# A gated three-branch decoder layer on one core: the RWKV state chain in whole-array matmuls, another order of the projection jobs, shorter roots, copies on ScalarE

## The chip, the cores and the metric

The kernel runs on one core of a Trainium2 chip. The metric is the device time of one execution in microseconds (us), as the median of several runs. Five engines work beside each other: TensorE (PE, matmuls and transposes), VectorE (DVE), ScalarE (ACT), GpSimd (POOL) and SyncE (SP), which issues most DMA transfers. Each engine works its instructions off in the order in which they stand in its program, and waits on semaphores for the others' results.

## What is computed

One layer over x of shape (1, 256, 2048), float32, between two RMS norms:

```python
h = rms_norm(x, norm_w)
proj = h @ w_in                       # 2048 -> 16592 columns
g_qkv, g_z, g_b, g_a, r_feat, r_z, s_u, s_z, gate_logits = split(proj)
o_a = gdn_branch(...)     # gated delta rule, 8 heads of 128, conv of 4 taps on q, k, v, chunks of 64
o_b = rwkv7_branch(...)   # RWKV-7 time mixing, 16 heads of 64, token shift on r, k, v
o_c = s5_branch(...)      # diagonal state space model, 64 groups of 16
merged = sum_b sigmoid(gate_logits_b + gate_b) * (o_b @ w_branch_b)
x = x + merged @ w_out
return rms_norm(x, final_norm_w)
```

The RWKV recurrence is S_t = S_{t-1} (diag(w_t) - kk_t^T (a_t kk_t)) + v_t^T k_t, y_t = S_t r_t, with a state of 64 x 64 a head. Almost all arithmetic is in the three projections (w_in, w_branch, w_out); the branches are many small steps.

## The kernel before, in words

**Projections.** A weight block is loaded by a DMA into a tile raw (128 x 1024 floats). ACT rounds it to a shorter format (whi, line 260), DVE takes the rest (wlo = raw - whi, line 261). Each projection product is three matmuls: whi by the upper part of the activations, whi by the lower, wlo by the upper. They are the tiles mm in the profile, 128 x 256 each, some 8,000 of them, and they are the filling between all other work of PE. A unit is one raw tile (24 matmuls), and a job is the two units of one block of 128 output columns (one unit where the activations have 1024 rows). When a job's last matmul is done, its callback takes the result out of PSUM: got_conv (a causal convolution of 4 taps, one ACT operation and three DVE passes of 255, 254 and 253 columns, tiles gc), got_shift (the token shift of r, k, v), got_z, got_gate and so on.

**Branches as lanes.** The small steps of the branches are Python generators in lanes ("g" for a head of the delta rule, "r" for a pair of RWKV heads, "i" for the inversion that both share, "t", "g2", "r2"). After every second k block of a job, pump() lets each lane whose count is due take one step; the number that a step yields is how many pumps it waits for the next. All of PE's matmuls are kept in the written order (class InOrder). The instructions of the other engines are put in order by a scheduler, and so a change of one edit moves instructions at many places.

**Rounds.** For each of 8 rounds r, front() brings the jobs q, k, v of head r, its gate z, then r, k, v of RWKV pair r and its gate z. After the job gz a new delta-rule head begins (ag), after rz a new RWKV pair (ar). NG = 9 gate jobs follow the rounds (front_gates), then the jobs of the third branch's input (front_su). Then the pool of the first two branches is closed and the third branch begins: its parameters come by DMA (s5raw, s5ldt) into memory that was the first branches', DVE copies s5ldt (line 1289), and PE transposes them (s5t).

**The RWKV state chain.** One pair of heads lies on 128 partitions, head 0 on rows 0 to 63, head 1 on rows 64 to 127. For each of four chunks c of 64 steps it does: rc (KR by the state, from the second chunk; its sum on DVE is rpn, line 998), rd (rpn by Mr), whose result goes into UV (one half by ACT, one by DVE, line 1005), and re (BKt by UV, up to the third), from which DVE makes the next state MS (rMS, lines 1016 and 1018). Each of rc, rd and re is two matmuls of 64 rows and 64 columns of the array, one for each head, on two quadrants of it. ra, a part of the pair's preparation, and ryo, its output, are matmuls of one head each as well.

**Roots.** rsqrt (line 118) starts from an estimate out of the float's bits, in two operations, and improves it in two rounds of three or four; it is called for the norm of x at the start (2 columns), the norms in the branches and the last norm (1 column).

**Head.** x is loaded in four pieces (xs), its squares are summed on ACT and DVE, the root is taken, the diagonal matrices are made from it (sc, line 228), and PE multiplies x by them (xtp, a transpose and a scaling in one), which gives the activations hT.

Of the kernel before, what the change touches and what calls it, by code (L numbers as in the profile page):

```python
# [18 lines left out]
P = 128  # L19
# [17 lines left out]
def tile_trunk(  # L37
# [80 lines left out]
    def rsqrt(o, v, n, parts=P, pool=None):  # L118

        qi = small(n, parts, I32, pool, bufs=4)  # L120
        ve.tensor_scalar(out=qi, in0=v.bitcast(I32), scalar1=1, scalar2=None, op0=ALU.logical_shift_right)
# [4 lines left out]
        g = (9 / 64) ** 0.12  # L126
        for c in (g * g, 64 / 9 * g ** 10):
            if n <= 2:
                for e in range(n):
                    e = slice(e, e + 1)  # L130
                    ve.scalar_tensor_tensor(out=w[:, e], in0=o[:, e], scalar=o[:, e], in1=v[:, e], op0=ALU.mult,
                                            op1=ALU.mult)
            else:
                ve.tensor_tensor(out=w, in0=o, in1=o, op=ALU.mult)
                ve.tensor_tensor(out=w, in0=w, in1=v, op=ALU.mult)
            ve.scalar_tensor_tensor(out=t, in0=w, scalar=-10 / 3 * c, in1=w, op0=ALU.add, op1=ALU.mult)
            ve.scalar_tensor_tensor(out=o, in0=t, scalar=5 * c * c, in1=o, op0=ALU.add, op1=ALU.mult)
# [80 lines left out]
    squares(1, 0, 1024, 0, ve)  # L218
    squares(0, 1024, 2048, 1, se)
# [190 lines left out]
    hlw = cp.tile([P, 16], F32, name="hlw")  # L410

    def parameters():
# [7 lines left out]
        ve.tensor_scalar(out=oka, in0=pv("ka", 0, 8), scalar1=-1.0, scalar2=1.0, op0=ALU.mult, op1=ALU.add)  # L420
# [145 lines left out]
    def inverse(r, TMc):  # L566
# [12 lines left out]
        for e in range(2):  # L579
            ve.tensor_scalar(out=T16[:, :, 16 * e:16 * e + 16], in0=TMc, scalar1=rmask[:, e:e + 1], scalar2=None,  # L580
                             op0=ALU.mult)
# [65 lines left out]
        ve.tensor_copy(Y.rearrange("p u j -> p (u j)"), py[0:64, 0:P])  # L647
# [130 lines left out]
    def gdn_tail(h):  # L778
# [15 lines left out]
        ve.tensor_copy(ot[:, 0], po[:, 0:P])  # L794
# [74 lines left out]
    def rwkv_pair(i):  # L869
# [12 lines left out]
        ve.tensor_scalar(out=lw, in0=lw, scalar1=-RW_C, scalar2=-RW_C, op0=ALU.mult, op1=ALU.add)  # L882
        ve.tensor_scalar(out=av, in0=av, scalar1=0.5, scalar2=0.5, op0=ALU.mult, op1=ALU.add)
# [14 lines left out]
        ve.tensor_scalar(out=ns, in0=pr[0:2, 0:T], scalar1=EPS, scalar2=None, op0=ALU.add)  # L898
# [10 lines left out]
        ve.scalar_tensor_tensor(out=bt, in0=k, scalar=pv("kk", i), in1=av, op0=ALU.mult, op1=ALU.mult)  # L909
        for h, sl in ((0, 0), (1, 2)):  # L910
            hp = slice(64 * h, 64 * h + 64)
            ve.tensor_tensor(out=BK[hp, :, sl], in0=ch4(bt)[hp], in1=ch4(en)[hp], op=ALU.mult)
# [819 lines left out]
```

## Time and profile before

| | |
|---|---|
| time, median of 3 runs | 1202.21 us (1201.90 to 1202.29) |
| the profiled execution | 1201.51 us, of which the span from first to last instruction is 1199.8 us |
| PE busy | 1177.0 us (98%) |
| DVE, ACT, POOL busy | 955.3 (80%), 619.1 (52%), 52.4 us (4%) |
| mean granted TensorE clock | 0.998 |
| DMA | 203.98 MB, mean 170 GB/s |

The span has a head up to the first projection matmul at 17.46 us, a stretch in which PE streams, and a tail from its last matmul at 1191.0 us. The rounds lie between about 60 and 640 us, the third branch and the remaining projections behind them. PE is the busiest engine by far; a row "PE a <- DVE b" in the view of waits is time in which PE had nothing to do until DVE had made b. In the timeline the durations of PE's matmuls overlap, because a matmul is in the array while the next one starts; what one costs is read from start to start.

### The profile page before, as it was taken

Reading aid. Unit: us, or ns where it says so; the run is one execution under the profiler, and the core shown is the slowest. Engines: PE = TensorE matmul, PEld = TensorE weight load, DVE = VectorE, ACT = ScalarE, POOL = GpSimd, SP = SyncE. Lnnn points to the kernel's source line nnn. Section 1 sums busy time; section 2 is a strip of 40 time slices with the busy share of each in tenths; the row PEclk is TensorE's granted clock in tenths of the full one; section 3 lists DMA queues with packets and bytes.
Section 4 is the critical chain, followed back from the end, with each engine's and each line's share of the span. In section 5 each row is a group of like instructions: output and inputs, shape, how many; then the busy total and the mean of one; then the engine's idle time right before and its main releaser. Section 6 shows DMA issues by size and latency. Waiting matters only on the chain. (4 is left out here: it accounts for less than half of the span.)

```text
span 1199.8 us, 29344 instructions
## 1 busy us (share of the span) xinstructions
PE 1177.0 (98%) x11670; PEld 1124.6 (94%) x11670; DVE 955.3 (80%) x2527; ACT 619.1 (52%) x1188; POOL 52.4 (4%) x92
## 2 busy tenths in 40 slices
PE   5999999999999999999999999999999999999997
PEld 5999999999999999999999999999999999999887
DVE  6879888889898898977558978999998765555555
ACT  5455656565555656564544554544444554444443
POOL 1000000000000000000002011111100000000000
PEclk9999999999999999999999999999999999999999
DMA  6766555555555555555557776777767666667763
GB/s 189 194 176 180 152 136 146 139 157 133 152 149 137 150 137 150 133 146 144 147 159 203 192 193 179 186 185 191 187 175 192 176 182 187 180 190 240 238 197 116
DMA packets 384643, 203.98 MB, mean 170 GB/s; under 512 B 38825, under 2 KB 376186, under 8 KB 384122
## 3 DMA queue, kind: packets, MB, share of 16 engines
q1 hardware_dynamic: 382650, 199.61, 61.4%
q8 instruction: 92, 1.51, 0.5%
q0 software_dynamic: 1536, 1.58, 0.5%
q10 hardware_dynamic: 320, 0.93, 0.2%
q14 instruction: 45, 0.37, 0.1%
HBM read 195.88 MB, written 6.18 MB: 168 GB/s over the span
## 5 line engine op out<-in xcount | busy, mean ns | idle before, releaser
L62 PE MATMUL mm<-hT,whi 128*128 128x256 f32 (+1 forms) x4160 | 781.5, 288 | 0.5 <-ACT gate L1216 0.5
L62 PEld LDWEIGHTS mm<-hT,whi 128*128 128x128 f32 (+1 forms) x4160 | 644.4, 191 | 13.0 <-issue 1.2
L62 PE MATMUL mm<-hT,wlo 128*128 128x256 f32 (+1 forms) x2080 | 587.3, 282 | 0.4 <-DVE wlo L261 0.4
L260 ACT ACTIVATE whi<-raw 128x1024 fp32r<-128x1024 f32 (+1 forms) x346 | 364.7, 1055 | 361.7 <-PE mm L62 288.0
L261 DVE TENSOR_TENSOR wlo<-raw,whi 128x1024 fp32r<-128x1024 f32 (+1 forms) x346 | 421.6, 1219 | 150.1 <-ACT whi L260 148.3
L62 PEld LDWEIGHTS mm<-hT,wlo 128*128 128x128 f32 (+1 forms) x2080 | 396.4, 191 | 0.6 <-DVE wlo L261 0.6
L62 PE MATMUL mm<-oT,whi 128*128 128x256 f32 x768 | 140.4, 283 | 0.0
L62 PEld LDWEIGHTS mm<-oT,whi 128*128 128x128 f32 x768 | 118.9, 191 | 0.4 <-issue 0.4
L62 PE MATMUL mm<-oT,wlo 128*128 128x256 f32 x384 | 108.4, 282 | 0.0
L62 PE MATMUL mm<-whi,mT 128*128 128x512 f32 (+1 forms) x288 | 76.8, 354 | 0.0
L62 PEld LDWEIGHTS mm<-oT,wlo 128*128 128x128 f32 x384 | 73.2, 191 | 0.2 <-DVE wlo L261 0.2
L62 PEld LDWEIGHTS mm<-whi,mT 128*128 128x128 f32 x288 | 51.2, 189 | 7.5
L62 PE MATMUL mm<-wlo,mT 128*128 128x512 f32 (+1 forms) x144 | 50.9, 354 | 0.0
L554 DVE TENSOR_TENSOR ivp<-ivZ,ivX 48x1 f32<-48x1 f32 (+14 forms) x120 | 34.4, 287 | 1.4
L673 DVE SCALAR_TENSOR_TENSOR gc<-mm,pv,gc 128x255 f32<-128x255 f32 (+2 forms) x72 | 34.0, 472 | 0.9 <-ACT gc L671 0.3
L62 PEld LDWEIGHTS mm<-wlo,mT 128*128 128x128 f32 x144 | 27.2, 189 | 3.8
L556 DVE TENSOR_REDUCE ivZ<-ivp 48x1 f32<-48x1 f32 (+14 forms) x120 | 27.3, 227 | 1.5
L62 PE MATMUL mm<-ysp,whi 128*128 128x256 f32 x128 | 22.8, 281 | 0.0
L1216 ACT ACTIVATE gate<-mm,hgate 128x256 f32<-128x256 f32 x48 | 22.1, 461 | 0.3
L1226 DVE SCALAR_TENSOR_TENSOR gate<-gate,mm 128x256 f32<-128x256 f32 x32 | 13.4, 417 | 11.2 <-PE mm L62 11.1
L62 PEld LDWEIGHTS mm<-ysp,whi 128*128 128x128 f32 x128 | 19.6, 188 | 0.0
L676 ACT ACTIVATE gth<-gc 128x256 f32<-128x256 f32 x24 | 9.8, 409 | 16.5 <-DVE gc L673 13.0
(534 smaller groups left out, 1248.2 us busy)
## 6 DMA issues: line engine op xcount, KB each, us to landing
raw<-in_w_in_dram SPq DMA_DIRECT2D x256, 512.0 KB, 3.8
raw<-in_w_branch_dram SPq DMA_DIRECT2D x48, 512.0 KB, 3.9
raw<-in_w_out_dram SPq DMA_DIRECT2D x32, 512.0 KB, 4.6
raw<-in_s_glu_w_dram SPq DMA_DIRECT2D x8, 512.0 KB, 4.0
xs<-in_x_dram SPq DMA_DIRECT2D x4, 512.0 KB, 7.5
xr<-in_x_dram SPq DMA_DIRECT2D x2, 1024.0 KB
raw<-in_w_in_dram SPq DMA_DIRECT2D x4, 384.0 KB
gr<-grow SPq DMA_DIRECT2D x8, 128.0 KB, 3.0
```

Of the source, the lines that this page charges most:

```text
L62: return self.put(nc.tensor.matmul(*a, **k).ins)
L260: u["top"] = lambda: se.activation(out=hi[:, 0:nn], in_=raw[:, 0:nn], func=AF.Copy)
L261: u["sub"] = lambda eng=ve: eng.tensor_tensor(out=lo[:, 0:nn], in0=raw[:, 0:nn], in1=hi[:, 0:nn].bitcast(F32), op=ALU.subtract)
L554: ve.tensor_tensor(out=pi, in0=Z[:, 0:i, 0:i].rearrange("p j c -> p c j"), in1=X[:, i, 0:i].unsqueeze(1).to_broadcast([8 * NU, i, i]), op= ...
L556: ve.tensor_reduce(out=Z[:, i, 0:i], in_=pi, axis=AX.X, op=ALU.add)
L673: ve.scalar_tensor_tensor(out=c[:, s:T], in0=p[:, 0:T - s], scalar=pv("cw", (3 - s) * 24 + col), in1=c[:, s:T], op0=ALU.mult, op1=ALU.add)
L676: se.activation(out=th, in_=c, func=AF.Tanh, scale=0.5)
L1216: se.activation(out=t, in_=pss[0][:, 0:T], func=AF.Tanh, scale=0.5, bias=hgate[:, b * 16 + i:b * 16 + i + 1])
L1226: ve.scalar_tensor_tensor(out=g, in0=g, scalar=1.0, in1=p0, op0=ALU.add, op1=ALU.mult)
```

## The change

- In the state chain rc, rd and re become one matmul each over all 128 rows. Mr and a new tile KKd (the keys of chunks 1 to 3) are block-diagonal, 128 x 128, with zeros off the diagonal; re multiplies both heads' blocks at once, 128 x 128, of which the two diagonal blocks are used. UV and BKt are laid out with the head inside the chunk for it. rMS is then two operations of 64 partitions.
- The order of the jobs in a round becomes q k v, r k v, then both gates z (in round 0 r k v, then q k v). The head begins after v of q k v, the pair after v of r k v.
- The root is one operation for its first estimate and a polynomial of three steps.
- A dozen kinds of copy and scaling go from DVE to ACT (ivTM, ivY, Tg, Mr, got, rUV, ryn, rlw, rns, rav, CX and others); the convolution accumulates in a part of scr rather than a tile of its own.
- 24 transposes of x into an unused bank are added to the head (warm), 8 of the first tile and 16 of the second.
- NG is 6; four more silu gates of the third branch get a tile of another pool.

```diff
     def rsqrt(o, v, n, parts=P, pool=None):
-        qi = small(n, parts, I32, pool, bufs=4)
-        ve.tensor_scalar(out=qi, in0=v.bitcast(I32), scalar1=1, scalar2=None, op0=ALU.logical_shift_right)
-        ve.tensor_scalar(out=o.bitcast(I32), in0=qi, scalar1=-1.0, scalar2=1594614160.0,
+        ve.tensor_scalar(out=o.bitcast(I32), in0=v.bitcast(I32), scalar1=-0.5, scalar2=1595560640.0,
                          op0=ALU.mult, op1=ALU.add)
...
+        p = w
+        for c in (-3.858316985510428, 6.076014067655522, -5.060410064109184):
+            ve.scalar_tensor_tensor(out=t, in0=p, scalar=c, in1=w, op0=ALU.add, op1=ALU.mult)
+            p = t
+        ve.scalar_tensor_tensor(out=o, in0=t, scalar=2.843571401280689, in1=o, op0=ALU.add, op1=ALU.mult)
...
+    def warm(i, n):
+        pw_ = br_bank("warm")
+        for j in range(n):
+            pe.transpose(pw_[:, 0:P], i, ident)
+
+    warm(xs[0][:, D - P:D], 8)
+    warm(xs[1][:, D - P:D], 16)
...
-    Mrs = [fp.tile([P, 4, 64], F32, name=f"Mr{i}") for i in range(2)]
+    Mrs = [fp.tile([P, 4, P], F32, name=f"Mr{i}") for i in range(2)]
+    KKd = fp.tile([P, 3, P], F32, name="KKd")
...
-            ve.tensor_scalar(out=T16[:, :, 16 * e:16 * e + 16], in0=TMc, scalar1=rmask[:, e:e + 1], scalar2=None,
-                             op0=ALU.mult)
+            se.activation(out=T16[:, :, 16 * e:16 * e + 16], in_=TMc, func=AF.Copy, scale=rmask[:, e:e + 1])
...
-                c = ft([P, T], "gc", f"gc{kind}{h}")
+                c = scr[:, 4]
...
+        for h in range(2):
+            hp = slice(64 * h, 64 * h + 64)
+            se.activation(out=KKd[hp, :, hp], in_=KR[hp, 1:4, 0], func=AF.Copy)
         for c in range(4):
             if c:
                 pc = br_bank(f"rc{i}{c}")
-                for h in range(2):
-                    hp = slice(64 * h, 64 * h + 64)
-                    pe.matmul(pc[hp, 0:64], lhsT=KR[hp, c, 0], rhs=MS[hp, c - 1], start=True, stop=True)
+                pe.matmul(pc[:, 0:64], lhsT=KKd[:, c - 1], rhs=MS[:, c - 1], start=True, stop=True)
                 ve.tensor_tensor(out=pn[:, c], in0=pc[:, 0:64], in1=pn[:, c], op=ALU.add)
                 yield 4
             pc = br_bank(f"rd{i}{c}")
-            for h in range(2):
-                hp = slice(64 * h, 64 * h + 64)
-                pe.matmul(pc[hp, 64:128], lhsT=Mm[hp, c], rhs=pn[hp, c], start=True, stop=True)
-            se.activation(out=UV[0:64, 0, c], in_=pc[0:64, 64:128], func=AF.Copy)
-            ve.tensor_copy(UV[64:128, 1, c], pc[64:128, 64:128])
+            pe.matmul(pc[:, 64:128], lhsT=Mm[:, c], rhs=pn[:, c], start=True, stop=True)
+            se.activation(out=UV[0:64, c, 0], in_=pc[0:64, 64:128], func=AF.Copy)
+            se.activation(out=UV[64:128, c, 1], in_=pc[64:128, 64:128], func=AF.Copy)
             yield 3
             if c < 3:
                 pc = br_bank(f"re{i}{c}")
+                pe.matmul(pc[:, 0:P], lhsT=BKt[:, c].rearrange("p h t -> p (h t)"),
+                          rhs=UV[:, c].rearrange("p h t -> p (h t)"), start=True, stop=True)
...
                 for h in range(2):
                     hp = slice(64 * h, 64 * h + 64)
-                    pe.matmul(pc[hp, 128:192], lhsT=BKt[:, h, c], rhs=UV[:, h, c], start=True, stop=True)
...
+                    ec, d = ep[hp, c, 64:65], pc[hp, hp]
+                    if c:
+                        ve.scalar_tensor_tensor(out=MS[hp, c], in0=d, scalar=ec, in1=me[hp], op0=ALU.mult, op1=ALU.add)
+                    else:
+                        ve.tensor_scalar(out=MS[hp, c], in0=d, scalar1=ec, scalar2=None, op0=ALU.mult)
...
-            for kind in range(3):
-                yield from job_cols(W, [(C_QKV + 1024 * kind + c, P)], got_conv(kind, r), hmov)
-            yield from job_cols(W, [(C_GZ + c, P)], got_z(gz, "gz", r), hmov, after=ag)
-            for kind, base in enumerate((C_R, C_K, C_V)):
-                yield from job_cols(W, [(base + c, P)], got_shift(kind, r), hmov)
-            yield from job_cols(W, [(C_RZ + c, P)], got_z(rz, "rz", r), hmov, after=ar)
+            def rkv():
+                for kind, base in enumerate((C_R, C_K, C_V)):
+                    yield from job_cols(W, [(base + c, P)], got_shift(kind, r), hmov,
+                                        **({"after": ar} if kind == 2 else {}))
...
+            for jobs in ((qkv, rkv) if r else (rkv, qkv)):
+                yield from jobs()
+            yield from job_cols(W, [(C_GZ + c, P)], got_z(gz, "gz", r), hmov)
+            yield from job_cols(W, [(C_RZ + c, P)], got_z(rz, "rz", r), hmov)
...
-    NG = 9
+    NG = 6
```

**How it moves DVE's instructions.** The last instructions of DVE up to rMS3, the state of pair 3 after re32 (rc32, rd32 and re32 are the visits of its third chunk; wlo are the lower parts of weight blocks, ivp and ivZ steps of the inversion, rUV the copy of rd32, scr convolution passes, gdj and gv steps of head 5). Before:

```order
L1005 COPY rUV3_4516<-rd32_5663 64x64
L556 TENSOR_REDUCE ivZ4_5454<-ivp4_5460 48x12
L261 TENSOR_TENSOR wlo96_5719<-raw96_5716,whi96_5718 128x1024
L554 TENSOR_TENSOR ivp4_5460<-ivZ4_5454,ivX4_5366 48x169
L736 SCALAR_TENSOR_TENSOR ges5_5759<-gr5_5590,gcol_233,posm_169 128x128
L556 TENSOR_REDUCE ivZ4_5454<-ivp4_5460 48x13
L734 SCALAR_TENSOR_TENSOR get5_5758<-gr5_5590,gcol_233,negm_164 128x128
L554 TENSOR_TENSOR ivp4_5460<-ivZ4_5454,ivX4_5366 48x196
L1016 SCALAR_TENSOR_TENSOR rMS3_5348<-re32_5710,rep3_4100,rme32_5713 128x64
```

And now:

```order
L268 TENSOR_TENSOR wlo93_5582<-raw93_5579,whi93_5581 128x1024
L570 TENSOR_TENSOR ivp4_5278<-ivZ4_5272,ivX4_5186 48x196
L688 SCALAR_TENSOR_TENSOR scr_77<-mm90_0_5412,pv0_224,scr_77 128x255
L572 TENSOR_REDUCE ivZ4_5272<-ivp4_5278 48x14
L688 SCALAR_TENSOR_TENSOR scr_77<-mm90_0_5412,pv0_224,scr_77 128x254
L570 TENSOR_TENSOR ivp4_5278<-ivZ4_5272,ivX4_5186 48x225
L688 SCALAR_TENSOR_TENSOR scr_77<-mm90_0_5412,pv0_224,scr_77 128x253
L572 TENSOR_REDUCE ivZ4_5272<-ivp4_5278 48x15
L737 SCALAR_TENSOR_TENSOR gdj5_5524,sm111_5523<-gg5_5520,ident_87 128x128
L699 SCALAR_TENSOR_TENSOR gv5_5503<-gth25_5501,scr_77 128x256
L737 SCALAR_TENSOR_TENSOR gdj5_5524,sm111_5523<-gg5_5520,ident_87 128x128
L1034 SCALAR_TENSOR_TENSOR rMS3_5169<-re32_5527,rep3_3947,rme32_5529 64x64 x2
```

The masks get and ges of head 5 went behind rMS3, and the convolution of head 5's third job (mm90) and its gv came in front of it. The whole stretch from rpn3 (after rc32) to rMS3 has 17 instructions between the two before, one wlo among them; now it has 24, with three wlo and six convolution passes (those of mm88 and mm90).

**How it moves PE's instructions.** PE at the same place, from the last matmuls of ra4 (preparation of the next pair) on. Before:

```order
L62 MATMUL ra4_5699<-rUV4_5551,rg040_5269 64x64
L62 MATMUL ra4_5699<-rUV4_5551,rg041_5273 64x64
L62 MATMUL re32_5710<-rUV3_4516,rBt3_4513 64x64 x2
L62 MATMUL mm96_0_5722<-hT0_75,whi95_5653 128x256
L62 MATMUL mm96_0_5722<-hT1_76,whi95_5653 128x256
```

And now:

```order
L62 MATMUL ra4_5505<-rUV4_5364,rg040_5092 64x64
L62 MATMUL ra4_5505<-rUV4_5364,rg041_5096 64x64
L62 MATMUL gg5_5520<-gqk5_5251 128x256 x2
L62 MATMUL re32_5527<-rUV3_4348,rBt3_4345 128x128
L62 MATMUL mm92_0_5539<-hT0_75,whi91_5457 128x256
```

gg5, the products of head 5's q and k, now stands between ra4 and re32, and re32 is one matmul of 128 columns. From rc32 to rc33 there are 60 projection matmuls in both. At the end of the rounds, from rq7 (a transpose of the last pair's output) to s5t, there are 90 projection matmuls before and 42 now.

More of the change, by code (lines that the diff above doesn't have):

```diff
@@ L125, in rsqrt @@
         t = small(n, parts, pool=pool)
[L126 to L137, printed above, removed]
+        if n <= 2:
+            for e in range(n):
+                e = slice(e, e + 1)
+                ve.scalar_tensor_tensor(out=w[:, e], in0=o[:, e], scalar=o[:, e], in1=v[:, e], op0=ALU.mult,
+                                        op1=ALU.mult)
+        else:
+            ve.tensor_tensor(out=w, in0=o, in1=o, op=ALU.mult)
+            ve.tensor_tensor(out=w, in0=w, in1=v, op=ALU.mult)
+        p = w
[3 more added lines that the diff above has]
+        ve.scalar_tensor_tensor(out=o, in0=t, scalar=2.843571401280689, in1=o, op0=ALU.add, op1=ALU.mult)
     def exp_parts(v, n, parts=P, pool=None):
@@ L410, in tile_trunk @@
     hlw = cp.tile([P, 16], F32, name="hlw")
+    hkk = cp.tile([P, 8], F32, name="hkk")
+    hka = cp.tile([P, 8], F32, name="hka")
+    cst = cp.tile([P, 2], F32, name="cst")
+    ve.memset(cst[:, 0:1], -RW_C)
+    ve.memset(cst[:, 1:2], EPS)
     def parameters():
@@ L793, in gdn_tail @@
         ot = ft([P, 2, P], "g2", f"got{h}", bufs=2)
-        ve.tensor_copy(ot[:, 0], po[:, 0:P])
+        se.activation(out=ot[:, 0], in_=po[:, 0:P], func=AF.Copy)
         yield 2
@@ L897, in rwkv_pair @@
         ns = ft([2, T], "rns", f"rns{i}")
-        ve.tensor_scalar(out=ns, in0=pr[0:2, 0:T], scalar1=EPS, scalar2=None, op0=ALU.add)
+        se.activation(out=ns, in_=pr[0:2, 0:T], func=AF.Identity, bias=cst[0:2, 1:2])
         nD = dp.tile([4, 2, 64], F32, tag="nD", name=f"nD{i}")
@@ L980, in rwkv_pair @@
                 kp = slice(64 * (1 - h), 64 * (1 - h) + 64)
-                pe.matmul(pa[hp, c * 64:(c + 1) * 64], lhsT=gh[h][kp, c], rhs=UV[kp, h, c], start=True, stop=True)
+                pe.matmul(pa[hp, c * 64:(c + 1) * 64], lhsT=gh[h][kp, c], rhs=UV[kp, c, h], start=True, stop=True)
         pn = ft([P, 4, 64], "rpn", f"rpn{i}", bufs=2)
@@ L1029, in rwkv_tail @@
             for c in range(4):
-                pe.matmul(yo(h, c), lhsT=gm[h][:, c], rhs=UV[:, h, c], start=c < 2, stop=c == 0,
+                pe.matmul(yo(h, c), lhsT=gm[h][:, c], rhs=UV[:, c, h], start=c < 2, stop=c == 0,
                           skip_group_check=True)
@@ L1047, in rwkv_tail @@
         rsqrt(rs, var, 4)
+        nm = small(4)
+        ve.scalar_tensor_tensor(out=nm, in0=mv[:, :, 0], scalar=-1.0, in1=rs, op0=ALU.mult, op1=ALU.mult)
         yn = ft([P, 4, 64], "r2", f"ryn{i}", bufs=2)
         for a in range(4):
-            ve.tensor_scalar(out=yn[:, a], in0=ysl[a], scalar1=mv[:, a, 0:1],
-                             scalar2=rs[:, a:a + 1], op0=ALU.subtract, op1=ALU.mult)
+            se.activation(out=yn[:, a], in_=ysl[a], func=AF.Identity, scale=rs[:, a:a + 1], bias=nm[:, a:a + 1])
         yield 7
@@ L1571, in s5_tile @@
         se.activation(out=y2, in_=y1, func=AF.Square)
-        ve.tensor_scalar(out=y2, in0=y2, scalar1=0.044715, scalar2=1.0, op0=ALU.mult, op1=ALU.add)
-        ve.tensor_tensor(out=y2, in0=y2, in1=y1, op=ALU.mult)
-        se.activation(out=y2, in_=y2, func=AF.Tanh, scale=math.sqrt(2.0 / math.pi))
+        ve.scalar_tensor_tensor(out=y2, in0=y2, scalar=1.0 / 0.044715, in1=y1, op0=ALU.add, op1=ALU.mult)
+        se.activation(out=y2, in_=y2, func=AF.Tanh, scale=0.044715 * math.sqrt(2.0 / math.pi))
         yield 1
@@ L1604, in f @@
             se.activation(out=th, in_=p0, func=AF.Tanh, scale=0.5)
-            sz[i] = gp.tile([P, T], F32, tag="gate", bufs=NG, name=f"sz{i}")
+            if i < N_SZ // 2:
+                sz[i] = mp.tile([P, T], F32, tag="sz", bufs=N_SZ // 2, name=f"sz{i}")
+            else:
+                sz[i] = gp.tile([P, T], F32, tag="gate", bufs=NG, name=f"sz{i}")
             ve.scalar_tensor_tensor(out=sz[i], in0=th, scalar=1.0, in1=p0, op0=ALU.add, op1=ALU.mult)
```

56 lines of the change are left out of this document (29 added, 27 removed).

## The prediction

> **What bounds the kernel now.** I read the busy times of the whole span and the waits of TensorE (PE) first, then the busy times by stretch, then single rows of the timeline at the places that the change touches. The first row of the page (busy us, share, instructions):
>
> ```profile
> PE 1177.0 (98%) x11670; PEld 1124.6 (94%) x11670; DVE 955.3 (80%) x2527; ACT 619.1 (52%) x1188; POOL 52.4 (4%) x92
> ```
>
> The waits (engine, the instruction that waited, its releaser: us in total, times, longest):
>
> ```profile
> PE xtp L62 <- DVE sc L228: 9.0, 1, 9.0
> ...
> PE mm L62 <- ACT gate L1216: 0.5, 1, 0.5
> ```
>
> The busy times of the rounds' middle (us of the span; length; busy time and instructions of PE, PEld, DVE, ACT, POOL; clock, DMA share, GB/s):
>
> ```profile
> 300.00:500.00 200.00, 200.00 (x2193) 187.08 (x2192) 178.24 (x574) 116.68 (x269) 5.63 (x6) 1.00 0.55 143
> ```
>
> After the head PE waits for almost nothing: the longest wait there is 0.5 us, and here it is busy 200.00 of 200.00 us while the vector engine (DVE) is busy 178 and the scalar engine (ACT) 117. So the end is set by what PE's instructions occupy one after the other, from the first projection matmul to the last, and by a head and a tail in which PE does not stream. A term of the change counts if it shortens what PE occupies, shortens head or tail, or makes PE wait. What DVE and ACT save counts only through the third, and there it matters where the few instructions stand for which PE waits.
>
> **The state chain on PE.** Rows of the timeline (start, us, engine, line, tiles, shape, records), with projection matmuls (mm) in groups of one wlo and two whi:
>
> ```profile
> 284.05 0.28 PE L62 MATMUL mm<-hT,wlo 128*128 128x256 f32 x1
> 284.17 0.60 PE L62 MATMUL g<-gS,gqk 128*128 128x128 f32 x4
> ...
> 284.85 0.28 PE L62 MATMUL mm<-hT,wlo 128*128 128x256 f32 x1
> ...
> 285.21 0.28 PE L62 MATMUL mm<-hT,wlo 128*128 128x256 f32 x1
> 285.42 0.33 PE L62 MATMUL rc<-rMS,rKR 64*64 64x64 f32 x4
> 285.68 0.50 PE L62 MATMUL mm<-hT,whi 128*128 128x256 f32 x2
> 286.02 0.28 PE L62 MATMUL mm<-hT,wlo 128*128 128x256 f32 x1
> ```
>
> Durations overlap here, so I take start to start. From 284.85 to 285.21 lie three mm: 0.36, 0.12 each. From 284.05 to 284.85 lie three mm and the whole-array g of four passes: 0.80 - 0.36 = 0.44, 0.11 a pass. From 285.21 to 286.02 lie three mm and one visit rc on two quadrants, again four passes: 0.81 - 0.36 = 0.45, of which its passes have 0.26 (285.42 to 285.68). The other 0.19 goes on the way to the quadrants and back. The pieces rd and re are of the same kind:
>
> ```profile
> L62 PE MATMUL rd<-rpn,Mr 64*64 64x64 f32 x128 | 10.6, 242 | 0.0
> L62 PE MATMUL re<-rUV,rBt 128*64 128x64 f32 x96 | 8.1, 246 | 0.0
> L62 PE MATMUL rc<-rMS,rKR 64*64 64x64 f32 x96 | 8.0, 242 | 0.0
> ```
>
> At four records a visit that is 32 + 24 + 24 = 80 visits. Each becomes one matmul over all 128 rows, two passes: 2 x 0.11 = 0.22. With 0.455 a visit (the rows are rounded) that saves 0.235, by 80: 18.8 us. A part is given back, since the quadrant matmuls ra remain:
>
> ```profile
> 302.82 0.68 PE L62 MATMUL ra<-rUV,rg 64*64 64x64 f32 x16
> 303.43 0.34 PE L62 MATMUL re<-rUV,rBt 128*64 128x64 f32 x4
> ```
>
> After ra the visit re has its 0.27 and nothing on top. Before, seven of the eight runs of ra are followed by a visit re or rd, and the way is paid once for both. In the new order six are followed by gg and one by the new re, both whole-array, so ra pays it itself: 7 x 0.2 = 1.4. What remains is **-17.4 us**. Bounds: the 56 new visits rd and rc have 64 columns, not g's 128. If a pass costs the 0.065 of a quadrant visit (0.26 / 4), they save 56 x 2 x 0.045 = 5 more. If the way back stays for some reason, the gain is near none (a rival below).
>
> **What the merge and the order of jobs put in the way.** In the rounds one stage of the chain runs rc2, rd2, re2, rc3, and PE's rc3 needs rMS of DVE, which needs re2. In the new DVE order 24 instructions stand between rpn (after rc2) and rMS (after re2), in rounds 1 to 5 alike. The same link before:
>
> ```profile
> 296.67 0.33 PE L62 MATMUL rc<-rMS,rKR 64*64 64x64 f32 x4
> 306.37 0.33 PE L62 MATMUL rc<-rMS,rKR 64*64 64x64 f32 x4
> ```
>
> ```profile
> 296.85 1.21 DVE L261 TENSOR_TENSOR wlo<-raw,whi 128x1024 fp32r<-128x1024 f32 x1
> 297.99 0.21 DVE L998 TENSOR_TENSOR rpn<-rc,rpn 128x64 f32<-128x64 f32 x1
> ...
> 298.36 0.47 DVE L827 SCALAR_TENSOR_TENSOR gog<-gp,hgnw,gz 128x256 f32<-128x256 f32 x1
> 298.75 0.24 DVE L556 TENSOR_REDUCE ivZ<-ivp 48x10 f32<-48x100 f32 x1
> ...
> 304.08 0.28 DVE L1016 SCALAR_TENSOR_TENSOR rMS<-re,rep,rme 128x64 f32<-128x64 f32 x1
> ...
> 304.54 0.47 DVE L447 SCALAR_TENSOR_TENSOR scr<-mm,pv,scr 128x255 f32<-128x255 f32 x1
> 304.93 0.53 DVE L554 TENSOR_TENSOR ivp<-ivZ,ivX 48x225 f32<-48x225 f32 x1
> 305.39 0.33 DVE L736 SCALAR_TENSOR_TENSOR ges<-gr,gcol,posm 128x128 f32<-128x128 f32 x1
> ```
>
> There DVE takes 304.08 - 297.99 = 6.1 us from rpn to rMS, with one wlo between, and rc3 starts 2.0 us after rMS has ended (306.37 - 304.36), so nothing waits. In the new order the convolution passes of two jobs stand there too, and three wlo. Start to start: 3 wlo at 1.14 = 3.4; 6 convolution passes at 0.39 (304.54 to 304.93) = 2.3; four ivp and five ivZ, growing with each step, at about 0.38 and 0.25 (ivp has 0.46 at its largest, 304.93 to 305.39, and ivZ 0.18 at the size 10) = 2.8; gog and oT, gqk, gv of the same size at 0.38 (298.36 to 298.75), and two gdj of half of it, = 1.9. With rpn 0.15 these make 10.5 us. Ahead of rpn lies rc2 with its way to DVE (0.4, an estimate from rc's 0.33), behind it rMS, now two instructions of 64 rows (0.4 for both, an estimate from 0.28 for one of 128), and the way to PE (0.3, an estimate): 11.7 us from rc2 to rc3. PE's own work between: 60 mm at 0.12 = 7.2, gp, rd, re and rc at 0.22 = 0.9, ra 0.6 + 0.2, gg in four passes of 256 columns 0.88 (twice g's, an estimate): 9.8 us. So PE waits 1.9 us, five times: **+9.5 us**. Bounds: 0, if DVE, which loses 266 of its 2511 instructions (at its mean of 955.3 / 2527 = 0.38 us some 100 us in all), is through more of the 24 before rc2 ends; but they stand behind rpn in its queue, and the convolutions' input comes from PE's own mm. And 3.0 each, were each of the 24 a tenth longer: 0 to +15.
>
> The copies that go from DVE to ACT cost nothing by themselves: ACT is busy 117 of 200 us. One of them, ivTM, puts a DMA's landing in ACT's way, with rUV and whi queued behind it. On DVE the wait for it was 0.3 us for 12 of them (60 to 500 us of the span):
>
> ```profile
> L580 DVE TENSOR_SCALAR ivTM<-ivT,rmask 128x96 f32<-128x96 f32 x12 | 4.6, 397 | 0.3 <-DMA ivT<-zD 0.3
> ```
>
> I take 0 for it; ACT, less loaded, may arrive there earlier and wait longer, which stays inside the bounds above.
>
> **The gate jobs.** Fewer gate jobs (NG 9 to 6) stand between rq of the last pair and s5t: 42 mm in the new PE order, 90 before. The chain between:
>
> ```profile
> L65 PE MATMUL s5t<-ident,s5raw x3: 221/223/247, 641.6 to 641.8; 32*128 32x32 f32 x3
> L1284 SPq DMA_DIRECT2D s5raw<-in_s_a_re_dram x1: 517/517/517, 635.1 to 635.1; - x1
> ...
> L1289 DVE COPY s5raw<-s5ldt x1: 228/228/228, 640.3 to 640.3; 32x128 f32<-32x128 f32 x1
> ```
>
> ```profile
> 630.54 0.38 PE L65 MATMUL rq<-ident,ryn 128*128 128x128 f32 x2
> ```
>
> The DMA waits for the last read of the tiles whose memory it takes (ryt, rog and oT after rq), then the landing, then DVE's copy, and s5t could have started near 640.6, 10 us after rq; without the wlo that stands ahead of the copy on DVE, 9 us. Now PE has 42 x 0.12 + 0.2 = 5.2 us of work there: **+3.8 us** (2.8 to 4.8: one less if ACT and DVE, less loaded, pass rq's result on sooner, one more with the full 10). PE idle that long meets the clock:
>
> ```profile
> 1191.00:1192.00 1.00, 0.01 (x1) 0.00 (x0) 0.42 (x1) 0.49 (x2) 0.00 (x0) 1.00 1.00 400
> ...
> 1193.00:1194.00 1.00, 0.00 (x0) 0.00 (x0) 0.82 (x6) 0.09 (x1) 0.00 (x0) 0.97 0.00 0
> 1194.00:1195.00 1.00, 0.00 (x0) 0.00 (x0) 0.99 (x2) 0.95 (x1) 0.00 (x0) 0.50 0.00 0
> ```
>
> PE's last matmul ends with 1191.0, and 3 us later the clock (third from the end) is at half. A cold start is priced by the head:
>
> ```profile
> 13.34 4.36 PE L62 MATMUL xtp<-sc,xs 128*128 128x128 f32 x24 [9.02 <-DVE sc L228]
> 17.46 0.48 PE L62 MATMUL mm<-hT,whi 128*96 128x256 f32 x2
> ```
>
> 24 passes took 17.46 - 13.34 = 4.1 us against 24 x 0.11 = 2.6: 1.5 us. I take half of it at s5t: **+0.7**.
>
> **Head and tail.** The root of x stands ahead of xtp:
>
> ```profile
> 11.04 0.17 DVE L121 TENSOR_SCALAR sm<-sm 128x2 int32<-128x2 int32 x1
> ...
> 13.00 0.48 DVE L228 TENSOR_SCALAR sc<-ident,sm 128x128 f32<-128x128 f32 x2
> ```
>
> Ten instructions in 1.96 us; seven remain, 0.59 us less, so xtp can start at 12.75. The added transposes take the last columns of the two tiles of x, whose second halves were read as they landed:
>
> ```profile
> 8.42 1.06 ACT L213 ACTIVATE sc<-xs 128x1024 f32<-128x1024 f32 x1 [2.51 <-DMA xs<-in_x_dram]
> 9.84 0.69 DVE L214 SCALAR_TENSOR_TENSOR junk<-xs 128x512 f32<-128x512 f32 x1 [1.80 <-DMA xs<-in_x_dram]
> ```
>
> The 8 of the first tile start at 8.4 and take 1.8 us cold, so the 16 of the second, landed at 9.8, follow without a gap. They end near 12.6 if the clock rises 3 us after the first (14 at 0.22, half the rate, and 10 at 0.11). Then xtp is warm and ends at 15.4, the first mm waits for hT of DVE to about 15.75 (xtp's end and the 0.3 of a handover, an estimate): **-1.7 us** (-2.0 to +0.4, the last if they stay cold and end at 13.7). The last root falls from eight instructions to six at 0.19, on the path that ends the kernel: **-0.4**.
>
> The Trainium skill (TensorE: Matmul & The Clock Gate, Part 4: PE-mode transpose) has a rule against this: transposes in PE's transpose mode do not count as busy for the clock, so that full rate does not engage. No run here shows it yet.
>
> **Sum**, against the profiled execution's 1201.5 (the median of three is 1202.2): 1201.5 - 17.4 - 1.7 - 0.4 + 9.5 + 3.8 + 0.7 = **1196 us**.
>
> **Rivals.** *No new waits*: DVE's link is shorter than I add it up, and the gate chain with it. For it: DVE has 100 us less to do; against: the 24 instructions stand in one queue. 1201.5 - 19.5 + 3 for s5t alone = 1185; chance 0.23. *Cold head*: the transposes do not raise the clock; everything else as forecast, 1196 + 2.1 = 1198.1; chance 0.13. The Trainium skill's rule above says that it goes this way. No row speaks for or against it, since before no run of transposes stands on an idle PE. *Clock lost in every round* (slower): what I price at s5t happens at rc3. It decides from a wait of 3 us, where the clock rows fall to half; the link would have to take 12.8 us instead of 11.7. Then 5 x (1.1 + 1.5) = 13 more: 1209; chance 0.10. *The merge removes nothing*: the way back belongs to the small tiles, not to the quadrants, and is still paid by mm. Then the 18.8 are gone, 1215; but the four passes of g are followed by mm with no such loss; chance 0.04. The forecast itself has 0.50, with a range of 1190 to 1201.
>
> **How the numbers follow.** Range 1184 to 1204: it takes in the forecast, the cold head and the upper half of the case without waits, and leaves out the rest of that (0.1), most of the lost clock and the empty merge (0.1). A measurement of this kernel can tell about 0.2% (2.4 us) from no change. Faster by more: most of the forecast's 0.50 (0.45), of the cold head (0.09), and all of the case without waits: 0.77. Slower: the lost clock, the empty merge less their milder ends (0.11). The same: 0.12.
>
> **What would show it.** In the profile of the changed kernel: rd, rc and re with 160 records and mm after them at the normal 0.12; in the waits of PE rc <- DVE rMS five times near 1.9 us, and s5t once near 3.8; xtp near 12.8 with its 24 records in 2.7 us; mm from 15.8. If the rMS wait is missing, the time is near 1185 and the sum of DVE's link was wrong; if rMS has waits of 3 us and mm behind them at twice 0.12, it is the slower case.

## The result, and the profile after

The changed kernel takes 1214.36 us (median of six runs, 1209.19 to 1217.58) against 1202.25 (1201.90 to 1202.61): ratio 1.010, interval 1.0085 to 1.0115. It is **slower by 1%**, where I had forecast 1196 with 1184 to 1204 around it. The six runs of the changed kernel lie 8.4 us apart, those of the kernel before 0.7. The profiled execution is the fastest of the six, 1209.19 us with a span of 1207.5.

The waits of TensorE in the changed kernel:

```profile
PE rc L62 <- DVE rMS L1034: 15.1, 6, 3.4
...
PE s5t L65 <- DMA raw<-in_w_branch_dram: 3.9, 1, 3.9
PE s5t L65 <- DVE s5raw L1315: 0.3, 1, 0.3
```

Both waits of the forecast are there. s5t has 4.2 us (forecast 3.8). rc has 14.8 us in the five rounds, and 0.3 once elsewhere: 3.35, 2.90, 2.55, 2.63 and 3.38, where I had 1.9 each. The row of s5t names the DMA of a weight block; s5t reads s5raw, whose two transfers were issued 4.7 and 2.9 us before it started, and the row of waits doesn't tell them apart. The busy times by stretch show the same as missing PE time (columns as before: PE, PEld, DVE, ACT, POOL, clock, DMA share, GB/s):

```profile
300.00:500.00 200.00, 191.17 (x2109) 182.90 (x2107) 161.06 (x474) 134.12 (x340) 6.56 (x6) 1.00 0.54 140
...
620.00:640.00 20.00, 15.69 (x106) 15.23 (x105) 11.02 (x39) 6.71 (x11) 7.56 (x13) 0.83 0.53 144
```

Between 300 and 500 us PE was busy 200.00 and is busy 191.17, though DVE's load has fallen from 178 to 161 us. The clock is 0.83 behind the wait of s5t. It also falls in the rounds. The first wait of rc ends at 230.24; the stretches of 1 us from there, and 2 us from the fifth wait on:

```profile
230.20:231.20 1.00, 0.96 (x8) 0.96 (x9) 0.95 (x4) 0.48 (x2) 0.00 (x0) 1.00 0.04 11
231.20:232.20 1.00, 1.00 (x8) 1.00 (x7) 0.68 (x4) 0.98 (x2) 0.00 (x0) 0.61 0.00 0
232.20:233.20 1.00, 1.00 (x7) 1.00 (x6) 0.64 (x1) 0.94 (x3) 0.00 (x0) 0.50 0.60 79
233.20:234.20 1.00, 1.00 (x7) 1.00 (x6) 0.79 (x2) 0.37 (x1) 0.00 (x0) 0.50 0.34 86
234.20:235.20 1.00, 1.00 (x8) 1.00 (x8) 0.00 (x0) 0.00 (x0) 0.00 (x0) 0.68 0.16 39
```

```profile
492.50:494.50 2.00, 1.98 (x16) 1.98 (x17) 1.64 (x7) 1.47 (x3) 0.00 (x0) 1.00 0.24 28
```

After the first wait PE runs at half clock from 231.4 to 234.8, where the clock's column (third from the end) reads 0.50. After the fifth, just as long, the clock stays at 1.00. The profile counts PE as busy all that time: the loss is in no row of waits, only in the clock's column. Of the five waits of this execution two are followed by such a stretch of 3.4 us, and s5t by one of twice that, 6.8 us.

Why the second of two waits of 3.4 us goes free is in the same trace. The clock changes at 231.42, 234.84, 296.28, 299.69, 630.78 and 637.61 us: all of these times lie whole multiples of 3.413 us apart (231.42 to 296.28 is 19 of them, 231.42 to 630.78 is 117). So I cut the time of PE into pieces of 3.413 us that start at these changes. The rows are the piece before the first fall and the piece of the fall, then the two pieces that share the fifth wait, then the stretch behind s5t:

```profile
228.01:231.42 3.41, 1.18 (x10) 1.18 (x11) 3.29 (x15) 1.11 (x3) 0.00 (x0) 1.00 0.55 160
231.42:234.84 3.42, 3.42 (x19) 3.42 (x18) 1.89 (x5) 2.07 (x5) 0.00 (x0) 0.50 0.29 53
487.42:490.84 3.42, 1.72 (x15) 1.51 (x13) 3.42 (x8) 0.00 (x0) 0.00 (x0) 1.00 0.85 214
490.84:494.25 3.41, 1.73 (x14) 1.73 (x15) 3.21 (x15) 1.64 (x4) 0.00 (x0) 1.00 0.45 117
630.78:637.61 6.83, 6.49 (x30) 6.32 (x31) 4.37 (x19) 1.06 (x1) 2.51 (x5) 0.50 0.40 101
```

The first wait leaves PE busy for 1.18 us of one piece, and the next piece has half clock. The fifth wait is as long, but a border of two pieces cuts it in half, each piece keeps 1.7 us of work, and the clock stays. Cut in the same way, the profiled executions of all fourteen kernels of this document agree, from the clock's first rise to PE's last matmul: each of the 18 pieces at full clock in which PE was busy 1.51 us or less is followed by half clock, and each of the others (1.55 us and more) by full clock.

At half clock half the time is lost: 13.7 us at half cost 6.8 us in the profiled run. The mean clock gives the price roughly, (0.998 - 0.993) x 1207.5 = 6 us; its last digit is worth 1.2 us, and it also counts the tail, where PE is idle. The six runs with their mean clocks:

| time, us | 1209.19 | 1211.50 | 1214.12 | 1214.59 | 1216.62 | 1217.58 |
|---|---|---|---|---|---|---|
| mean granted clock | 0.993 | 0.990 | 0.987 | 0.987 | 0.984 | 0.984 |

The time follows the clock: 0.009 of it is 11 us by the same sum, and 8.4 us lie between the ends. The likely reading is that the runs differ in how many of the waits the clock falls behind, as the borders of the pieces lie elsewhere against the waits in each run; only the profiled run has a trace that shows it.

The state chain's matmul and the times of head and tail came out as forecast. Rows around rd, and around the head:

```profile
220.19 0.28 PE L62 MATMUL mm<-hT,wlo 128*128 128x256 f32 x1
220.31 0.33 PE L62 MATMUL rd<-rpn,Mr 128*128 128x64 f32 x2
220.45 0.48 PE L62 MATMUL mm<-hT,whi 128*128 128x256 f32 x2
220.77 0.28 PE L62 MATMUL mm<-hT,wlo 128*128 128x256 f32 x1
```

```profile
8.26 5.11 PE L65 MATMUL warm<-ident,xs 128*128 128x128 f32 x24 [3.99 <-DMA xs<-in_x_dram]
13.21 2.84 PE L62 MATMUL xtp<-sc,xs 128*128 128x128 f32 x24
15.81 0.48 PE L62 MATMUL mm<-hT,whi 128*96 128x256 f32 x2
```

From wlo to wlo are 0.58 us with three mm in them: the visit costs 0.58 - 0.36 = 0.22. The first mm starts at 15.81, not 17.46.

Together, for the profiled run: merge -17.4 (as forecast), head -1.65, tail -0.3, rc +15.1, s5t +4.2, clock +6.8 make +6.8 of the 7.7 us between the two spans. The other 0.9 us I have not assigned.

### The profile page after: what moved, and what is told of

Same layout as the page of the kernel before. It is cut to its first block, busy times and chain, and to the rows that moved or that the text cites. A ratio compares the mean times of both kernels' runs of the same rounds, so it can differ in the third digit from the quotient of the medians.

```text
span 1207.5 us, 29032 instructions
## 1 busy us (share of the span) xinstructions
PE 1171.0 (97%) x11534; PEld 1131.5 (94%) x11534; DVE 908.8 (75%) x2261; ACT 679.4 (56%) x1412; POOL 54.7 (5%) x92
## 5 line engine op out<-in xcount | busy, mean ns | idle before, releaser
L62 PE MATMUL mm<-oT,whi 128*128 128x256 f32 x768 | 143.2, 287 | 0.0
L688 DVE SCALAR_TENSOR_TENSOR scr<-mm,pv,scr 128x255 f32<-128x255 f32 (+2 forms) x72 | 33.7, 469 | 0.1
L691 ACT ACTIVATE gth<-scr 128x256 f32<-128x256 f32 x24 | 9.9, 412 | 24.3 <-DVE scr L688 24.3
L62 PE MATMUL rc<-rMS,KKd 128*128 128x64 f32 x48 | 8.8, 265 | 15.1 <-DVE rMS L1034 15.1
L62 PEld LDWEIGHTS rc<-rMS,KKd 128*128 128x128 f32 x48 | 7.5, 194 | 16.3 <-DVE rMS L1034 15.8
```

What stands on the lines that cost most here:

```text
L62: return self.put(nc.tensor.matmul(*a, **k).ins)
L688: ve.scalar_tensor_tensor(out=c[:, s:T], in0=p[:, 0:T - s], scalar=pv("cw", (3 - s) * 24 + col), in1=c[:, s:T], op0=ALU.mult, op1=ALU.add)
L691: se.activation(out=th, in_=c, func=AF.Tanh, scale=0.5)
```

## The experiments

Theory A throughout: DVE's queue in front of rMS makes rc wait, too little work stands ahead of s5t, and the clock falls behind the waits; what is left without them is the merge, the head and the tail.

**rms_first: rMS ahead in DVE's queue.** The order of one engine is set with an order-only dependence, which costs no wait. `held` has the first convolution pass of v and the fourteenth step of the inversion; the second wlo after rMS is held too.

```diff
+                        if c == 2 and h and 0 < i < 6:
+                            for ins in (held.pop("conv", None), held.pop("iv", None)):
+                                if ins is not None:
+                                    tc.add_manual_dep(ins, o.ins.name, NOSYNC, reason="order")
+                            gate_.update(wlo=o.ins.name, n=0)
```

> The changed kernel with one thing added: in rounds 1 to 5 DVE must do rMS of the third chunk ahead of the convolution of v, the last two steps of the inversion and the second wlo behind re. Theory A (the queue in front of rMS is the loss): the five waits rc <- rMS, 14.8 us in the profiled run, go, and with them the slow clock behind them, which in the runs of the changed kernel above the profiled one costs up to 8 us: 1192 to 1196 us against 1214.4. Rival B (DVE is late as a whole, and the wait only moves to what is held back: gv, wlo, rpn of the next chunk): the sum of PE's waits stays near 19 us and the time above 1208.

Measured: 1189.73 us (1188.75 to 1190.41), ratio to before 0.9898 (0.9881 to 0.9914). The waits:

```profile
PE s5t L65 <- DMA raw<-in_w_branch_dram: 3.6, 1, 3.6
PE rg L62 <- DVE scr L948: 0.3, 1, 0.3
PE rc L62 <- DVE rMS L1049: 0.2, 1, 0.2
```

Fifteen microseconds of rc are gone, and nothing has come in their place: theory A, and 24.6 us of time, since the clock no longer falls in the rounds. That is 2.3 us more than the range allowed. Rival B is out. Putting rMS, 0.6 us long, ahead of some nine others takes nothing from DVE's load, and it turned the change from 1% slower to 1% faster.

**s5late: s5t asked for later.** The lane yields 7 pumps, not 1, between the DMA's issue and s5t.

```diff
         nc.sync.dma_start(out=ldt, in_=s5_log_dt[0].rearrange("(i g) -> i g", g=2))
-        yield 1
+        yield 7
```

> The changed kernel with s5t asked for six pumps (36 mm, 4.3 us) later, nothing else. Theory A (s5t waits because too few mm stand between it and rq, and the clock falls behind the wait): the 3.9 us of wait and about 3 us of slow clock behind it go: 1207 to 1209 us. Rival B (the rest of the third branch's setup is then late by as much): a wait of 3 us or more appears in the stretch from 640 to 700 us, and the time stays at 1212 to 1215.

1207.07 us (1204.48 to 1209.11): 7.3 us less than the changed kernel. The wait of s5t fell to 0.5 us and the clock does not fall behind it, and nothing later waits instead: theory A. The five waits of rc are as they were (15.1 us), and in its profiled run the clock fell behind four of them, two of which were 2.6 and 2.7 us long, where in that of the changed kernel it fell behind two: the same waits, met by other borders.

**both: the two edits together.**

> Both of these edits together. Theory A: all waits of PE between head and tail are below 1 us each, the clock stays at 0.998, and what is left of the forecast's sum is the merge, the head and the tail: 1202.2 - 17.4 - 1.7 - 0.4 = 1182.7; I expect 1181 to 1186. Rival B (the merge saves nothing, and the waits hide it): near 1200. Rival C (waits move to other places): 1190 to 1205 with new rows in the waits.

1183.64 us (1183.32 to 1185.06), ratio to before **0.9849** (0.9835 to 0.9864). That is 0.9 us from the sum of the forecast without waits. No wait of PE between head and tail is above 0.5 us, the clock is at 0.998, and the runs lie 1.7 us apart: theory A, and neither of the rivals. It is the best version that I have, 1.5% faster than the kernel before and 2.5% faster than the change as it was made.

**oldord: the changed kernel with the old order of jobs.** The block that yields the jobs is that of the kernel before; all else is as changed.

> The changed kernel with the order of jobs as before (q k v, gate, r k v, gate, in every round, heads and pairs begun after their gates), everything else as changed. Theory A (it is the new order that puts two convolutions and three wlo in front of rMS): the waits rc <- rMS go, and 1195 to 1202 us remain, since the last pair ends later against the last jobs and rq or s5t may wait 4 to 9 us there. Rival B (the merged chain is what is too fast for DVE, whatever the order): the waits rc <- rMS stay at 2 us or more each, and the time at 1210 or more.

1203.66 us (1202.69 to 1205.88). The waits:

```profile
PE rq L65 <- ACT ryn L1069: 4.7, 1, 4.7
...
PE rc L62 <- DVE rMS L1034: 3.7, 4, 1.4
PE s5t L65 <- issue: 3.7, 1, 3.7
```

rc loses 11.4 of its 15.1 us, each wait being 1.4 at most and the clock staying up in the rounds. So the order of jobs made most of it. The old order pays elsewhere: 4.7 us at rq and, in three parts, 4.9 at s5t, with half clock behind both, 13.7 us in one stretch. The time is 1.7 us above the range that I gave. No run has the old order without these two waits, so what the new order gains by itself is not shown.

**before_ord: the kernel before with the new order alone.**

> The kernel before with the new order of jobs alone; state chain on quadrants, long roots, copies on DVE, nine gate jobs, as before. Theory A (the order of jobs alone puts the convolutions and three wlo in front of rMS): waits rc <- rMS of 2 to 4 us in rounds 1 to 5, the clock falling behind some of them, 1212 to 1226 us. Rival B (it takes the faster merged chain as well): no wait above 1 us, 1201 to 1205.

1227.33 us (1226.41 to 1228.84), 1.021 (1.0195 to 1.0226).

```profile
PE rc L62 <- DVE rMS L1016: 12.0, 7, 2.4
```

That is theory A, 1.3 us above its range. The order of jobs alone costs 25.5 us: 12.0 of rc (2.23 to 2.38 in each of the five rounds), some 3.4 of small waits that were not there, and 6.8 of clock (four stretches of 3.4 us at half). Some 3 us of it are not assigned. The clock fell behind four of the five waits, though each is shorter than the 3 us of my forecast; behind the one that ends at 304.2 it did not. There a border cut the wait, and PE was busy 1.65 us in the first piece; in the four others it was 1.50 or less.

**cover: more of PE's work in place of another order on DVE.** The changed kernel with s5t later, DVE's order untouched.

```diff
-                yield 3
+                yield 8 if c == 2 else 3
```

> The changed kernel with s5t later, as above, and with DVE's order left as the change has it: instead rc of the fourth chunk is asked for five pumps (30 mm, 3.6 us) later after re of the third. Theory A (what counts is DVE's stretch of 13.3 us from rc to rc against PE's work between, 9.9 us): the wait shrinks by the 3.6 us of cover to near zero, 1183.6 to 1187 us. Rival B (DVE is loaded further in the meantime and stays behind, whatever PE does): waits of 2 us and more remain, 1195 or more.

1193.10 us (1192.04 to 1194.77). The waits:

```profile
PE ivw L62 <- ACT Mg L650: 2.8, 5, 0.9
...
PE s5t L65 <- DMA raw<-in_w_in_dram: 2.4, 1, 2.4
...
PE rc L62 <- DVE rMS L1034: 0.3, 1, 0.3
```

The wait of rc went as theory A says: PE's work between is what DVE's stretch is held against. But by the edit the rest of the pair's chain comes 3.6 us later in every round, and I take this to be why ivw waits for ACT, rq waits 1.2 us, and s5t waits again, with the clock at half behind it. So the expected 1183.6 to 1187 was missed by 6 us. A later yield is not the same as an earlier instruction.

**rms_conv: the convolution alone behind rMS.** As both, without holding the second wlo and the inversion.

> The kernel with both edits, but with the convolution of v alone held behind rMS: the second wlo and the inversion's last steps are ahead of it again. Theory A (each instruction in front counts with its own start-to-start time): of the 5.3 us that stood between re and rMS some 1.5 us go (three passes and gv), so that the wait is near 1.5 us in each of five rounds with the clock up: 1190 to 1194. Rival B (the convolution, which waits for PE's own mm, was the whole cause): 1183 to 1186.

1200.55 us (1199.19 to 1204.14).

```profile
PE rc L62 <- DVE rMS L1047: 8.5, 5, 1.8
PE ivw L62 <- ACT Mg L661: 5.3, 5, 1.1
```

The waits of rc are 1.6 to 1.8 us each, as added up, and in the profiled run, one of the fastest, the clock stays at 1.00 behind each of them. It did not always: the slowest three of the ten runs, 1202.5 to 1204.1 us, have mean clocks of 0.995 and 0.996, which suggests that waits of this length can meet it too. What I had not expected are 5.3 us at ivw. So the time is not in 1190 to 1194: 1183.6 + 8.5 + 5.3 = 1197.4, and 3 us more, part of them the clock of the slower runs; the rest I can't assign. Rival B (the convolution as the whole cause) is out: the wlo and the inversion's steps in front of rMS count too.

**both_quad: the merge undone.** From the same tiles, each of rc, rd and re as two matmuls on its quadrants, for instance:

```diff
-                pe.matmul(pc[:, 0:64], lhsT=KKd[:, c - 1], rhs=MS[:, c - 1], start=True, stop=True)
+                for h in range(2):
+                    hp = slice(64 * h, 64 * h + 64)
+                    pe.matmul(pc[hp, 0:64], lhsT=KKd[hp, c - 1, hp], rhs=MS[hp, c - 1], start=True, stop=True)
```

> The kernel with both edits (rMS ahead, s5t later; 1183.6 us), and rc, rd and re again as two matmuls of one head each on their quadrants, from the same block-diagonal tiles; nothing else differs. Theory A (a visit costs 0.455 us, 0.19 of it for the way there and back, and the whole-array matmul 0.22): +17.4 us, 1199 to 1202. Rival B (the merge saves nothing, and the gain of the kernel with both edits comes from elsewhere): 1183 to 1187.

1204.08 us (1203.58 to 1204.64): +20.4. Of these 2.1 are new waits of ivw:

```profile
PE ivw L62 <- ACT Mg L663: 2.1, 5, 0.4
```

So the merge is worth 18.3 us, against 17.4 forecast, and the rival that it removes nothing is out. The time lies 2.1 us above the range, which had no new waits in it.

**both_nowarm: without the transposes.** The two calls of warm are taken out.

> The kernel with both edits (1183.6 us) without the 24 transposes in the head. Theory A (the transposes raise the clock for xtp): xtp starts some 0.8 us earlier, near 12.4, but takes 4.1 us again in place of about 2.6, and the first mm starts 0.7 to 1.3 us later: 1184.3 to 1185. Rival B (the transposes do not raise the clock, xtp does): the first mm starts 0.8 us earlier, 1182.8.

1186.90 us (1186.31 to 1187.56): +3.3. The head without them, and with them (both):

```profile
12.91 5.27 PE L62 MATMUL xtp<-sc,xs 128*128 128x128 f32 x24 [8.73 <-DVE sc L244]
17.94 0.36 PE L62 MATMUL mm<-hT,whi 128*96 128x256 f32 x1
```

```profile
8.55 5.38 PE L65 MATMUL warm<-ident,xs 128*128 128x128 f32 x24 [4.34 <-DMA xs<-in_x_dram]
13.73 2.88 PE L62 MATMUL xtp<-sc,xs 128*128 128x128 f32 x24
```

Without them xtp runs cold for all its 5.0 us and the first mm starts at 17.94; with them xtp takes 2.6 and mm starts at 16.37. That is 1.6 us in the head. The small waits behind it sum to 1.8 us here and 1.2 in both. Together that is 2.2 us, where the two profiled executions lie 1.9 apart (1186.95 and 1185.06); that of both is the slowest of its four, and 1.1 of the 3.3 us between the medians are not assigned. So theory A in kind, above its range in size.

**both_d5 and both_d14: what a wait costs.** Copies on DVE, 5 or 14, are forced between re and rMS of the third chunk in rounds 1 to 5.

```diff
+                    if c == 2 and h == 0 and 0 < i < 6:
+                        for q in range(5):
+                            last_ = ve.tensor_copy(dly, pc[:, 0:64])
```

> The kernel with both edits, with 5 copies of 64 columns on DVE (about 0.2 us each) forced between re and rMS of the third chunk in rounds 1 to 5. They make rc wait again, by 1 to 2 us each. Theory A (a wait costs its own length, and the clock only after waits near 3 us): the time is 1183.6 plus the sum of the waits read from the profile, 1189 to 1193, with the clock at 0.998. Rival B (every wait at this place costs a slow stretch behind it, whatever its length): 1.5 us more for each, 1197 to 1200.

> The same with 14 copies: waits near 4 us, five times. Theory A: 20 us of wait, and behind every wait the clock at half for 1.5 to 3 us, which costs half of that each: 1183.6 + 20 + 5 x 1.5 to 3 = 1211 to 1219, mean clock 0.98 to 0.985, and little spread between runs, since every wait is long enough. Rival B (the clock falls at random, in 2 to 4 of 5, as in the changed kernel): 1206 to 1212 with a spread of 5 us and more.

With 5 copies 1194.19 us (1193.29 to 1195.81), +10.6; with 14, 1213.55 (1212.63 to 1214.49), +29.9. The waits with 5, then with 14:

```profile
PE ivy L62 <- DVE sm L141: 6.1, 5, 1.2
...
PE ivw L62 <- ACT Mg L664: 1.3, 5, 0.3
PE rc L62 <- DVE rMS L1056: 1.3, 5, 0.5
```

```profile
PE rc L62 <- DVE rMS L1056: 14.9, 6, 3.2
...
PE ivw L62 <- ACT Mg L664: 3.6, 5, 1.3
```

With 5 most of the wait came at ivy instead of rc, 8.7 us in all in pieces of 1.2 and less, with the clock at 0.998: such waits cost little more than their length. So theory A, 1.2 us above its range. With 14 the waits of rc are 2.8 to 3.2 us and those of rc and ivw sum to 18.5; the other 11.4 us are the clock, with one stretch of 3.4 us at half and three of 6.8, which cost 11.9. It fell behind four of the five waits. Time and spread are those of theory A, but it had the clock fall behind every wait; that one of five goes free is rival B's. One of them ends at 363.85:

```profile
363.80:365.80 2.00, 1.95 (x9) 1.95 (x10) 1.94 (x5) 0.77 (x3) 0.00 (x0) 0.50 0.00 0
365.80:367.80 2.00, 2.00 (x11) 2.00 (x11) 2.00 (x6) 1.32 (x2) 0.00 (x0) 0.50 0.12 32
367.80:369.80 2.00, 2.00 (x12) 2.00 (x11) 1.83 (x5) 0.00 (x0) 0.00 (x0) 0.50 0.28 51
```

This makes the loss of the changed kernel again, in a kernel that has none, and with the same two parts.

**both_dve: eight copies back on DVE.** ivTM, Tg, ivY (two), Mr, got and the two of rUV, as tensor_copy or tensor_scalar on DVE as before.

> The kernel with both edits, with eight kinds of the copies moved to ACT back on DVE (ivTM, Tg, ivY, Mr, got, both of rUV). Theory A (such copies cost nothing where neither engine is late): within 2 us of 1183.6. Rival B (DVE needs the room that the copies made): waits of PE for DVE of 1 us and more a round, 1189 or more.

1186.12 us (1185.70 to 1186.33): +2.5, just outside the 2 us, with one new wait of 1.2 us at ivy and some of 0.2 to 0.4. These eight copies on ACT are worth little, as the prediction had it; the merge, the order of jobs and two positions in queues are what moves this kernel. The roots and NG were not undone one by one.

## Why the prediction was wrong

**What bounds the kernel**: right. Every difference above that is assigned is either time that PE's instructions occupy, or a wait of PE, or PE's clock. Of the 18.4 us between 1196 and the median, 5.6 are rc (15.1 for 9.5), 0.4 s5t, 6.1 the clock of the profiled run (6.8 for 0.7), and 5.2 what the median lies above that run; the other 1.1 are not assigned.

**The merge**: right, 18.3 us measured for 17.4. The bound of 5 us more for visits of 64 columns did not come.

**The wait of rc**: place and cause right, size wrong. The step that failed is "Ahead of rpn lies rc2 with its way to DVE (0.4 ...)". Rows of the changed kernel, first round of the five:

```profile
217.01 0.33 PE L62 MATMUL rc<-rMS,KKd 128*128 128x64 f32 x2
```

```profile
218.96 0.23 DVE L1015 TENSOR_TENSOR rpn<-rc,rpn 128x64 f32<-128x64 f32 x1
...
229.61 0.58 DVE L1034 SCALAR_TENSOR_TENSOR rMS<-re,rep,rme 64x64 f32<-64x64 f32 x2
```

```profile
230.24 0.43 PE L62 MATMUL rc<-rMS,KKd 128*128 128x64 f32 x2 [3.35 <-DVE rMS L1034]
```

From rpn to rMS are 10.65 us (10.5 added up), from rMS to rc 0.63 (0.7), and PE's work between the two rc took 13.23 - 3.35 = 9.9 (9.8). But from rc2 to rpn are 1.95 us, not 0.4: rpn stood behind ivp and ivZ. In the rows that I quoted of the kernel before it was already 297.99 - 296.67 = 1.3. I took the way of a signal for the way through a queue, where the trace had the number. With 1.95 the sum gives 3.4 us for this round, which is what was measured. In the five rounds rpn starts 1.95, 1.51, 1.14, 1.23 and 2.06 us after rc2, and the other terms are equal to 0.1 us in all of them: the waits of 3.35, 2.90, 2.55, 2.63 and 3.38 us differ by this term alone.

**The clock**: the step that failed is "It decides from a wait of 3 us". I read that off one place, the end of the kernel, where PE is idle for good, and so the forecast put the clock behind rc at nothing. In the traces the clock fell behind waits of 2.23 us upward (before_ord), in most cases but not all, and behind none of the fifteen waits of 1.0 to 1.8 us in rms_conv and both_d5. What decides in these traces is not the length of the wait but PE's work in one piece of 3.413 us, 1.51 us or less, which is 1.9 us idle. A wait below 1.9 us makes the clock fall only together with others in its piece, one of 1.9 to 3.8 us when a border does not cut it too evenly. With that, the changed kernel's five waits lie in the range where it may fall, and the cost is not a fixed one: 6.8 us in the fastest run, (0.998 - 0.984) x 1215 = 17 us by the mean clock in the slowest. The wait of s5t was sized rightly (4.2 for 3.8), its clock not: 6.8 us at half clock cost 3.4, for which I had 0.7, because 24 passes of the head (1.5 us lost) were taken as the price of a whole return.

The Trainium skill (TensorE: Matmul & The Clock Gate, Part 1: The HAM clock gate) gives an idle window of about 3.4 us, free-running, after which the clock is halved. The length and the free running agree with the traces here: changes lie multiples of 3.413 us apart, and waits of equal length end differently. But the window need not be idle throughout, since windows with up to 1.51 us of work were enough, and so were waits of 2.23 to 2.38 us, four times in five.

**The likeliest case and the rivals.** What came is the third rival, the clock lost in the rounds, which I gave 0.10 and 1209 us. It had the right mechanism and too low a chance, because the two wrong steps work together: a link longer by 0.7 to 1.6 us, and a clock that falls behind shorter waits. That its 1209 is the time of the fastest run is in part luck: it has a stretch at half clock behind all five waits, that run behind two of them and a longer one behind s5t. The case without waits is what the kernel with both edits shows, 1183.6; the rival's 1185 has 3 us for s5t in it, 1182 without.

**Head and tail**: 1.65 and 0.3 us, for 1.7 and 0.4. The cold head did not come. That the head's number fits so well is luck: the clock rose 4.7 us after the first transpose and not 3, so xtp started at 13.21 and not 12.75, and the first mm followed xtp's last pass without the 0.3 us of a handover that I had put there. In the tail DVE's shorter root brings the write of the result forward by 0.44 us; the time from the last matmul to the end is 8.8 us before, 8.4 here, and 8.8 again in the run both, with the same root, so not all of it reaches the end in every run. The rule of the Trainium skill that I set beside it (same page, Part 4: PE-mode transpose) does not hold for these transposes of 4-byte data: they start at 213 ns each, and in the profiled run of the changed kernel fall to 110 after 22 of them, 4.7 us from the first; xtp behind them has 112 from its first pass.

**The copies to ACT**: right within 2.5 us.

## What to carry to other kernels

Where one engine is busy all the time, ask of every instruction on which it waits what stands ahead of it in its own engine's queue, and add the whole stretch from the first signal to the last by rows, the queue at its start included. DVE had 46 us less to do (955.3 to 908.8; 266 fewer instructions took off 0.17 us each, where my 100 us had the mean of all, 0.38) and was later at the one place that mattered; most of the loss was undone by moving one step forward.

A wait of TensorE of about 2 us or more can have a second price that no row of waits shows: look at the clock in the microseconds behind it, and take runs that scatter as a sign of it. Short waits that lie close together add up.

## What the runs showed of the hardware

In these traces the clock of TensorE changes only at the borders of pieces of 3.413 us. It falls after a piece in which PE was busy 1.51 us or less and not after one of 1.55 us or more. In the head the clock came back after 3.0 to 4.9 us of work in the three traces without the transposes, and 3.8 to 6.0 in the eleven with them; behind a wait it stayed at half for 3.4 or 6.8 us, and for 13.7 behind the two waits that follow each other in oldord. One whole-array fp32 matmul of two passes costs 0.22 us between projection matmuls, and two on quadrants 0.455, for half the array's work: here filling the array with zeros is cheaper than using its quadrants one by one.
